# Loading the first 4096 columns of x in eight loads of every 8th partition

## The chip, the cores and the metric

The kernel runs on one core of a Trainium2 chip. The metric is device time in microseconds (us) of one execution, and lower is better. Each kernel was timed in rounds beside the kernel before on the same chip. The experiments used three chips, so their ratios are compared rather than their times.

## The reference

```python
batch, dim = 1024, 4096            # x, y: float32 (1024, 4096)
def reference(x, y, axis):         # axis = -1
    return np.sum((x - y) ** 2, axis=axis).astype(np.float32)
```

Two arrays of 16.8 MB are read, and 4 KB are written. There is one subtraction, one square and one addition for each pair of elements.

## The kernel before

Eight rows of the batch lie in each of the 128 partitions, as one line of 32,768 columns. x and y come in pieces of columns, large ones first and small ones at the end, so that little is left to compute after the last byte. VectorE (DVE in the profile) subtracts, and ScalarE (ACT) squares and sums. All loads are issued by the SyncEngine (SP), and each has a semaphore of its own.

```python
xv = x.rearrange("(p r) d -> p (r d)", p=P)        # P = 128
...
xw = [4096, 12288, 8192, 5472, 1280, 960, 320, 160]      # widths of the x loads
yw = [16256, 8192, 2624, 2784, 1344, 480, 480, 288]
...
def load(landed, src, dst, name, c0, c1):
    sem = prog.semaphore("%s%d" % (name, len(landed)))
    nc.sync.dma_start(out=dst[:, home(c0, c1)], in_=src[:, c0:c1]).then_inc(sem, 16)
    landed.append(((c0, c1), sem))
...
load(*todo.pop(0))                         # x, columns 0 to 4095
prog.early(mybir.EngineType.SP)            # ... moved ahead of the entry barrier
while todo and todo[0][5] <= H:            # H = 24576 columns of room
    load(*todo.pop(0))                     # x 12288, y 16256, x 8192, y 8192
```

`early` moves the instructions issued so far in front of the barrier at which all engines meet before the program's body. So the first load is under way while the engines still meet: its issue starts at 0.00 us and its first packet at 1.00, and the first issue behind the barrier starts at 1.43.

Of the kernel before, what the change touches and what calls it, by code (L numbers as in the profile page):

```python
# [47 lines left out]
def kernel(tc, x, y, axis, out):  # L48
    nc = tc.nc
# [10 lines left out]
    xv = x.rearrange("(p r) d -> p (r d)", p=P)  # L60
# [5 lines left out]
    X = nc.alloc_sbuf_tensor("X", [P, H], F32).ap()  # L66
# [24 lines left out]
    prog = Program(nc, tc)  # L91
# [6 lines left out]
    def home(c0, c1):  # L98
        h0 = c0 % H
        return slice(h0, h0 + c1 - c0)  # L100


    landed_x, landed_y = [], []
    freed = []

    def load(landed, src, dst, name, c0, c1):
        sem = prog.semaphore("%s%d" % (name, len(landed)))
        nc.sync.dma_start(out=dst[:, home(c0, c1)], in_=src[:, c0:c1]).then_inc(sem, 16)  # L108
        landed.append(((c0, c1), sem))
# [7 lines left out]
        order.append((landed_y, yv, Y, "y", c0, c1))  # L117

    todo = list(order)
    load(*todo.pop(0))  # L120
    prog.early(mybir.EngineType.SP)
    while todo and todo[0][5] <= H:
        load(*todo.pop(0))

# [21 lines left out]
    k = 0  # L146
# [5 lines left out]
    k = 0  # L152
# [10 lines left out]
    def wait_loaded(c1, ysem):  # L163

        waits = []
        while seen_x[0] < len(xs) and xs[seen_x[0]][0] < c1:
            waits.append(seen_x[0])
            seen_x[0] += 1
        nc.vector.wait_ge(ysem, 16)
        for k in waits:  # L170
            nc.vector.wait_ge(landed_x[k][1], 16)

    def sub(c0, c1):
        a = X[:, home(c0, c1)]
# [21 lines left out]
    for j, (c0, c1) in enumerate(ys):  # L196
        final = j == len(ys) - 1
        wait_loaded(c1, landed_y[j][1])
        for piece in pieces_of(j, c0, c1):
            sub(*piece)  # L200
            r = piece[0] // D
            if final:
                nc.vector.wait_ge(diffs, n["diffs"])
                nc.vector.tensor_tensor_reduce(  # L204
                    out=Y[:, home(*piece)],
                    in0=X[:, home(*piece)],
                    in1=X[:, home(*piece)],
                    scale=1.0,
                    scalar=parts_of(r, 1),
                    op0=mult,  # L210
                    op1=add,
                    accum_out=results[:, r : r + 1],
                ).then_inc(sums, 1)
                n["sums"] += 1
                continue
            square(*piece, where[piece])
            squared[piece] = n["acts"]
            if r in (0, 1):

                nc.sync.wait_ge(acts, n["acts"])  # L220
                while todo and todo[0][5] <= H + (r + 1) * D:
                    load(*todo.pop(0))
                if r == 1:
                    while todo:
                        load(*todo.pop(0))
# [43 lines left out]
```

## Time and profile before

| | before |
|---|---|
| median of 5 runs | 84.19 us (84.02 to 84.40) |
| span of the profiled run | 82.6 us |
| DVE, ACT busy | 45%, 40% |
| DMA queue, share of 16 engines | 95.9% |

The lines are in the prediction below. The table is to be read from its last row: the 16 DMA engines are filled nearly to the end, and the two compute engines idle for 40 us before the first large piece of y has landed. The time is the time of one stream of bytes, plus a start of 1 us and a tail of less than 3 us.

### The profile page before, as it was taken

How to read it: one execution, taken by the hardware profiler on the slowest of the kernel's cores; microseconds unless marked ns; L12 is line 12 of the kernel's file. 1: busy time of each engine (PE TensorE's matmuls, PEld its weight loads, DVE VectorE, ACT ScalarE, POOL GpSimd, SP SyncE). 2: the span in 40 equal slices, each digit the busy share in tenths (PEclk: the TensorE clock that was granted, in tenths of full speed). 3: DMA queues.
4: the chain of work that ended last, by engine and by line, in shares of the span. 5: the costliest groups of instructions: out<-in, count | busy, mean ns of one | idle time of the engine just before them, and what ended most of it. 6: DMA issues, size and time to landing. Idle time of an engine off the chain costs nothing.

```text
span 82.6 us, 136 instructions
## 1 busy us (share of the span) xinstructions
DVE 36.8 (45%) x27; ACT 33.4 (40%) x41; POOL 0.2 (0%) x4
## 2 busy tenths in 40 slices
DVE  0000000000000000000299999999189996989992
ACT  3300000000000000000000979889896999899991
POOL 0000000000000000000000000000000000000000
DMA  5998998888999991999599699969979799999960
GB/s 127 389 500 381 595 547 381 381 381 381 504 504 504 504 504 63 441 504 504 254 508 508 286 476 508 476 286 508 423 339 509 339 437 440 426 402 416 395 220 2
DMA packets 2736, 33.56 MB, mean 406 GB/s; under 512 B 432, under 2 KB 1328, under 8 KB 1712
## 3 DMA queue, kind: packets, MB, share of 16 engines
q1 hardware_dynamic: 2736, 33.56, 95.9%
HBM read 33.55 MB, written 0.00 MB: 406 GB/s over the span
## 4 chain that ended last, share of the span: by engine, by line
DMA 63%; SPq 16%; DVE 12%; ACT 4%; issue 1%
DMA Y<-in_y_dram 63%; SPq L108 16%; DVE X L175 11%; ACT X L181 4%; DVE Y L204 0%; DVE results L188 0%; SPq L220 0%; DVE results L204 0%
## 5 line engine op out<-in xcount | busy, mean ns | idle before, releaser
L175 DVE TENSOR_TENSOR X<-X,Y 128x2048 f32<-128x2048 f32 (+10 forms) x21 | 36.2, 1780 | 44.3 <-DMA Y<-in_y_dram 44.3
L181 ACT ACTIVATE X<-X 128x2048 f32<-128x2048 f32 (+9 forms) x20 | 31.2, 1559 | 46.1 <-DVE X L175 46.0
L181 ACT ACTIVATION_READ_ACCUMULATOR X<-X 128x1 f32 x20 | 3.7, 186 | 0.0
L181 ACT ACT_TABLE_LOAD x1 | 1.3, 1283 | 1.4 <-PEq L19 1.4
L188 DVE TENSOR_REDUCE results<-parts 128x1 f32<-128x2 f32 (+2 forms) x4 | 0.4, 152 | 0.0
L204 DVE CUSTOM_DVE_ANT_0 Y<-X,parts 128x128 f32<-128x128 f32 x1 | 0.4, 352 | 0.0
L250 POOL MEMSET const-bfloat16-1.0<- 128x1 bf16 x1 | 0.1, 101 | 0.0
L250 POOL MEMSET const-uint8-127<- 128x1 uint8 x1 | 0.1, 101 | 0.0
L250 POOL MEMSET const-float32-0.0<- 128x1 f32 x1 | 0.1, 98 | 0.2 <-issue 0.2
L250 POOL MEMSET const-float32-1.0<- 128x1 f32 x1 | 0.1, 98 | 0.0
L204 DVE DVE_READ_ACCUMULATOR2_ANT results<- 128x1 f32 x1 | 0.1, 83 | 0.0
## 6 DMA issues: line engine op xcount, KB each, us to landing
Y<-in_y_dram SPq DMA_DIRECT2D x1, 8128.0 KB, 39.0
X<-in_x_dram SPq DMA_DIRECT2D x1, 6144.0 KB, 20.2
X<-in_x_dram SPq DMA_DIRECT2D x1, 4096.0 KB, 48.3
Y<-in_y_dram SPq DMA_DIRECT2D x1, 4096.0 KB, 57.5
X<-in_x_dram SPq DMA_DIRECT2D x1, 2736.0 KB, 13.3
X<-in_x_dram SPq DMA_DIRECT2D x1, 2048.0 KB, 7.1
Y<-in_y_dram SPq DMA_DIRECT2D x1, 1392.0 KB, 19.0
Y<-in_y_dram SPq DMA_DIRECT2D x1, 1312.0 KB, 16.1
```

The costliest lines, as they stand in the source:

```text
L108: nc.sync.dma_start(out=dst[:, home(c0, c1)], in_=src[:, c0:c1]).then_inc(sem, 16)
L175: nc.vector.tensor_sub(out=a, in0=a, in1=Y[:, home(c0, c1)]).then_inc(diffs, 1)
L181: nc.scalar.activation(out=a, in_=a, func=Square, accum_out=acc).then_inc(acts, 1)
L188: nc.vector.tensor_reduce(out=results[:, r : r + 1], in_=parts_of(r, len(row_parts[r])), axis=mybir.AxisListType.X, op=add,).then_inc(sums, 1)
L204: nc.vector.tensor_tensor_reduce(out=Y[:, home(*piece)], in0=X[:, home(*piece)], in1=X[:, home(*piece)], scale=1.0, scalar=parts_of(r, 1), ...
L250: nc = _bacc.Bacc("TRN2", target_bir_lowering=False, num_devices=1)
```

## The change

The first x load, of 128 rows, shows in the trace of before as 128 packets of 16,384 bytes with 16 under way at a time: eight for each of 16 DMA engines. The change cuts the first x load into eight loads of 16 rows, one row (16 KB) for each engine. The intent is that an engine has its first packet, and the queue its first work, sooner. Three of the loads stand ahead of the barrier.

```diff
+    combed = [prog.semaphore("comb%d" % k) for k in range(8)]
+
+    def comb(k, c0, c1):
+        nc.sync.dma_start(out=X[k::8, home(c0, c1)], in_=xv[k::8, c0:c1]).then_inc(combed[k], 16)
...
-    load(*todo.pop(0))
+    c0, c1 = todo.pop(0)[4:]
+    landed_x.append(((c0, c1), None))
+    for k in range(3):
+        comb(k, c0, c1)
     prog.early(mybir.EngineType.SP)
+    for k in range(3, 8):
+        comb(k, c0, c1)
...
-            nc.vector.wait_ge(landed_x[k][1], 16)
+            for sem in [landed_x[k][1]] if k else combed:
+                nc.vector.wait_ge(sem, 16)
```

## The prediction

Passages are cut, and each cut is marked. They rested on rules of the hardware that no trace or run shows; the trace of before could not test them, since all its loads have 128 partitions.

> **What bounds the kernel now.** I read the page first: the slices, the DMA queue and the chain that ended last.
>
> ```profile
> span 82.6 us, 136 instructions
> DVE 36.8 (45%) x27; ACT 33.4 (40%) x41; POOL 0.2 (0%) x4
> DMA  5998998888999991999599699969979799999960
> q1 hardware_dynamic: 2736, 33.56, 95.9%
> HBM read 33.55 MB, written 0.00 MB: 406 GB/s over the span
> DMA 63%; SPq 16%; DVE 12%; ACT 4%; issue 1%
> ```
>
> The two compute engines are busy less than half of the span; the packets of the one DMA queue fill 95.9% of what 16 engines have in it. The zeros and fives in the DMA row are not pauses: packets of up to 65,024 bytes are counted in the slice where they start or end. So I asked for stretches instead (columns: stretch, its length, busy time of DVE, ACT and POOL, TensorE clock, DMA share, GB/s):
>
> ```profile
> 0.00:1.00 1.00, 0.00 (x0) 0.00 (x0) 0.20 (x4) 1.00 0.08 16
> 1.00:2.50 1.50, 0.00 (x0) 1.06 (x1) 0.00 (x0) 1.00 1.18 339
> 6.50:21.00 14.50, 0.00 (x0) 0.00 (x0) 0.00 (x0) 1.00 1.00 434
> 21.00:40.00 19.00, 0.00 (x0) 0.00 (x0) 0.00 (x0) 1.00 1.01 438
> 40.00:60.00 20.00, 17.30 (x4) 12.94 (x7) 0.00 (x0) 1.00 1.02 437
> 60.00:80.00 20.00, 18.43 (x18) 18.25 (x30) 0.00 (x0) 1.00 0.98 405
> 80.00:82.60 2.60, 1.08 (x6) 0.96 (x6) 0.00 (x0) 1.00 0.03 2
> ```
>
> The reader is to see three parts. Nothing moves in the first microsecond. Then there is a short ramp at 339 GB/s, and from there a stream at 434 to 438 GB/s that falls off only where the loads get small. The last part, 2.6 us, is the tail after the last byte. Single packet records of the trace say the same: the first packet starts 1.00 us into the span, the last of the 16 engines' first packets at 1.49; these first packets take 0.96 to 1.43 us, every later 16,384-byte packet of the first load 0.61 to 0.67, and each follows the one before it at once. The first load's last packet ends at 6.77 us, and I find no engine pausing from there to the last load's end at 79.87. The kernel is one DMA stream with a start and a tail; **what delays the stream delays the end by as much**.
>
> Last, the chain of waits in order of time, and the issues (size, time to landing):
>
> ```profile
> 1.43 0.33 SPq L108
> 1.81 39.02 DMA Y<-in_y_dram
> 53.45 0.33 SPq L108
> 66.94 13.12 DMA Y<-in_y_dram
> 80.08 0.57 DVE X L175 x2
> ...
> X<-in_x_dram SPq DMA_DIRECT2D x1, 2048.0 KB, 7.1
> ```
>
> The 2,048 KB load is the one that is changed. It does not stand in the chain by name: the chain passes from an issue at 1.43 us straight to the big y load, 39.02 us later. That is how the view draws a queue: the y load took 39 us because the first x load and a 6,144 KB load are ahead of it on the same engines. The changed load is thus on the path, through its place in the queue.
>
> [...]
>
> [...]
>
> [...]
>
> **The change part by part.** It removes one load of 128 rows x 16 KB. It adds 8 loads of 16 rows x 16 KB, three of them ahead of the entry barrier. No arithmetic changes; the listing of instruction order shows all engines but the issuing one as before.
>
> [...]
>
> Start. An issue takes 0.38 us in the first place, 0.43 to 0.44 in a row (starts 0.48 apart). The first packet at 1.00 us comes some 0.6 us after the first issue ends. With 16 rows, not 128, to describe, the spread of 0.49 us between the engines' starts may shrink. The ramp holds little: at 339 instead of 434 GB/s over 1.5 us it loses 1.5 x (1 - 339/434) = 0.33 us, most of it the cold first packets, which stay. I take **-0.15 us**.
>
> Issues. Two more loads ahead of the barrier put all three of its rounds off by 2 x 0.48, since the issuing engine is the last to come to its first round: the fourth load is issued at about 1.43 + 0.96 = 2.4 us. By then three packets per engine are queued, which last until about 1.0 + 0.65 + 3 x 0.61 = 3.5 us[...]; 2.4 + 0.6 = 3.0 is earlier. Then a load comes every 0.48 us, quicker than 0.61. The 6,144 KB load goes out near 4.8 us instead of 1.43, before the queue is empty. **0**.
>
> Completion. Seven more semaphore packets per engine: 9 ns each and about 6 to the next in the trace, 7 x 15 ns = **+0.1 us**. DVE has seven more waits ahead of its first subtraction. All of those loads land well before the y load of 39 us, whose wait stands last on that instruction: **0**.
>
> Later. DVE sits idle 40.86 us before its first subtraction; moving everything later by the same amount meets no other bound. Sum: 4.8 - 0.15 + 0.1 = +4.75 us; 84.19 + 4.75 = 88.9.
>
> **The rivals.** [...] Then only the start counts, between -0.3 and +0.1: 84.0 us. For it speaks that the kernel is finely tuned and the change's author expected a gain[...].
>
> [...]
>
> *C: the HBM side.* Neighbouring rows of one load lie 1 MiB apart (8 rows of 128 KiB). If such a step were read slower, it would add to A[...]. [...]
>
> **Range and chances.** [...] A real gain above 2% would need 1.7 us, more than the whole idle first microsecond and the ramp's 0.33, so 0.01. I predict 88.8 us and, to hold B, 86.0 to 89.6. Faster 0.01, same 0.2, slower 0.79.
>
> **What would show it.** Right: between about 1.5 and 11 us near 217 GB/s, packets of 16,384 bytes at about 1.22 us, the 6,144 KB load's packets starting near 11.3 instead of 6.55 us, and every later stretch as before but about 4.8 us later. A would show 0.61 us packets throughout and an x load done by 6.7 us. B would show 8 engines' packets at 0.61 us while the other 8 are still idle until about 3.5 us. A gap between packets of the first loads near 3 us would show that issue[...] is the bound. If the first stretch is slow and yet the end is not later, my claim that the stream has no slack is wrong.

The sum came to +4.75 us, and one of its terms, +4.8 us, was the estimate, not shown by any run at that time, that the first load would go at half rate: its 2.097 MB take 4.83 us at the measured 434 GB/s, and 9.67 at half of that. The other terms stand: -0.15 for the start, 0 for the issues, +0.1 for the completion. 84.19 + 4.75 = 88.9, put down as 88.8. Of the rivals, A says that the rate does not fall (84.0 us), and B that each load runs on half of the engines, so that the other half starts late (86.7); C is the step between the rows that are read. The chances were 0.7 for the half rate (88.3 to 89.5), 0.1 for B and a loss between (85.9 to 88), and 0.2 for A. The cuts in the expectations below have the same reason. A forecast that begins with a cut is that of the theory that the experiments test.

## The result, and the profile after

| | before | after |
|---|---|---|
| median of 5 runs | 84.19 us (84.02 to 84.40) | 89.05 us (88.94 to 89.08) |
| span of the profiled run | 82.6 us | 87.7 us |

The ratio is 1.0573, with a 95% interval of 1.0554 to 1.0592. A ratio here is the mean time of one kernel's runs over that of the other's runs of the same rounds, so it is not quite the ratio of the medians. The change made the kernel 5.7% slower.

From the page of the changed kernel:

```profile
span 87.7 us, 147 instructions
DVE 36.8 (42%) x27; ACT 33.4 (38%) x41; POOL 0.2 (0%) x4
q1 hardware_dynamic: 2848, 33.56, 95.6%
HBM read 33.55 MB, written 0.00 MB: 383 GB/s over the span
```

DVE and ACT did the same 36.8 and 33.4 us of work. The DMA queue is as full as before, 95.6%, but it moved 383 GB/s where it had moved 406. So the engines did not wait more, they were slower while busy. That is the first thing to take from these lines: *a busy share says nothing of the rate*.

The stretches show where. Their columns are the stretch, its length, busy time of DVE, ACT and POOL, TensorE clock, DMA share and GB/s. First the kernel before, from 4 to 10 us:

```profile
4.00:10.00 6.00, 0.00 (x0) 0.00 (x0) 0.00 (x0) 1.00 1.01 437
```

Then the changed kernel:

```profile
0.00:1.00 1.00, 0.00 (x0) 0.00 (x0) 0.20 (x4) 1.00 0.00 0
1.00:2.50 1.50, 0.00 (x0) 0.00 (x0) 0.00 (x0) 1.00 1.10 284
4.00:10.00 6.00, 0.00 (x0) 0.43 (x1) 0.00 (x0) 1.00 1.02 216
11.00:26.00 15.00, 0.00 (x0) 0.00 (x0) 0.00 (x0) 1.00 1.00 428
45.00:65.00 20.00, 17.30 (x4) 12.81 (x7) 0.00 (x0) 1.00 1.01 434
65.00:85.00 20.00, 18.34 (x18) 18.26 (x29) 0.00 (x0) 1.00 0.98 405
```

From 4 to 10 us the DMA share is the same 1.0, and the rate is 216 in place of 437: half. From 11 us on the numbers are those of before, five microseconds later. The view counts a packet as a whole where it falls, so a short stretch can be a few per cent off.

The chain of waits carries the same delay to the end:

```profile
6.82 39.14 DMA Y<-in_y_dram
58.58 0.33 SPq L114
72.44 12.72 DMA Y<-in_y_dram
85.18 0.57 DVE X L187 x2
```

The big y load took 39.14 us from issue to landing, and 39.02 before. But it was issued at 6.82 in place of 1.81, and so it landed 5.12 us later (45.96 against 40.84). The rest of the chain follows: the last subtractions start at 85.18 in place of 80.08. That the *issue* is late is not the cause, though it looks like it here. The y load's bytes come after those of both x loads on the same 16 engines (its first packet starts at 25.76 us, the 6,144 KB load's last at 24.49), and the experiments below that issue early and still lose show it.

Last, what the issuing engine and the barrier did (start, duration, engine, line, operation):

```profile
0.00 6.16 SPq L110 DMA_DIRECT2D X<-in_x_dram  x8
3.14 1.28 ACT L193 ACT_TABLE_LOAD   x1 [3.14 <-PEq L19]
```

ACT's table load stands right behind the barrier. It started at 1.44 us before and starts at 3.14 now: three issues of 0.57 to 0.59 us each, and a longer drain of the issuing engine (0.37 us, 0.13 before), stand in front of it.

For a finer measure I worked out, from the packet records of the traces, how many bytes had come by each moment, and when the kernel before had had as many. The difference is how far a kernel is behind; this number will be called **lag**:

| at (us) | 2.5 | 4 | 6 | 8 | 10 | 14 | 30 | 60 |
|---|---|---|---|---|---|---|---|---|
| lag of the changed kernel (us) | 0.13 | 0.81 | 1.84 | 2.79 | 3.83 | 4.81 | 4.84 | 4.91 |

It grows by half a microsecond per microsecond while the eight loads run, and stops when they are done. The last packet of all loads ends at 84.99 us in place of 79.87.

### The profile page after: what moved, and what is told of

It reads as the page before. It is cut to its first block, busy times and chain, and to the rows that moved or that the text cites. A ratio compares the mean times of both kernels' runs of the same rounds, so it can differ in the third digit from the quotient of the medians.

```text
span 87.7 us, 147 instructions
## 1 busy us (share of the span) xinstructions
DVE 36.8 (42%) x27; ACT 33.4 (38%) x41; POOL 0.2 (0%) x4
## 3 DMA queue, kind: packets, MB, share of 16 engines
q1 hardware_dynamic: 2848, 33.56, 95.6%
## 4 chain that ended last, share of the span: by engine, by line
DMA 59%; SPq 19%; DVE 11%; ACT 4%; issue 1%
DMA Y<-in_y_dram 59%; SPq L114 16%; DVE X L187 11%; ACT X L193 4%; SPq L110 3%; DVE Y L216 0%; DVE results L200 0%; SPq L232 0%; DVE results L216 0%
```

## The experiments

The theory: which partitions a load writes sets its rate, and the 16 of each of the eight loads give half. Why these should be slow together is not shown by any run. The rivals: the step of 1 MiB between the rows that are read (HBM side); the number of loads and issues; the shape of 16 rows as such; half of the engines idle at first (B of the prediction). Edits are against the changed kernel unless said otherwise. All results passed the comparison with the reference.

### Which side of the transfer

**e1_hbm_contig** reads 16 neighbouring rows of x but writes the same partitions. Its output is wrong, which doesn't matter for the time. Computed on the host, 126 sums are off by more than 0.01%, the worst by 7.7%, and the whole result by 0.9%.

```diff
-        ...(out=X[k::8, home(c0, c1)], in_=xv[k::8, c0:c1])
+        ...(out=X[k::8, home(c0, c1)], in_=xv[16 * k : 16 * k + 16, c0:c1])
```

> The eight loads still write every 8th partition, but each reads 16 neighbouring rows of x (steps of 128 KiB in place of 1 MiB); the sums are wrong on purpose. [...] nothing changes, 88.6 to 89.5 us, and packets of 16,384 bytes stay at about 1.2 us. Rival, the step of 1 MiB on the HBM side is what is read slowly: back to 84.2 to 85 us with packets near 0.61 us.

Measured: 89.03 us, ratio 1.0578 (1.0553 to 1.0604), the same as the change. The stretch from 4 to 10 us:

```profile
4.00:10.00 6.00, 0.00 (x0) 0.43 (x1) 0.00 (x0) 1.00 1.00 210
```

The HBM step falls. The same partitions written give the same half rate, whatever rows are read.

**e2_block16** takes 16 neighbouring partitions for each load, on both sides.

```diff
-        ...(out=X[k::8, home(c0, c1)], in_=xv[k::8, c0:c1])
+        p = slice(16 * k, 16 * k + 16)
+        ...(out=X[p, home(c0, c1)], in_=xv[p, c0:c1])
```

> Eight loads of 16 neighbouring partitions, both sides alike, right result. [...] HBM-step rival: 84.3. Rival that eight loads of 16 rows are slow as such: the same 89 us as the change.

The forecast gave 89.3 to 99 us, with packets near 2.4 us at the slow end.

Measured: 95.50 us, ratio 1.1345 (1.1322 to 1.1369).

```profile
4.00:10.00 6.00, 0.00 (x0) 0.00 (x0) 0.00 (x0) 1.00 1.02 128
```

The rate is 128 GB/s with all engines busy (DMA share 1.02); packets take 2.05 us, not 2.4, and the result lies in the range. Loads of the same number, rows and bytes as the change cost over twice as much extra. Neither their number nor their shape can explain that. Against e1 the pair is cleaner still: both read the same 16 neighbouring rows in each load, and only the partitions that are written differ, yet one takes 89.03 us and the other 95.50. It also shows that such a load can start as early as before: its first packet came at 0.99 us, while the changed kernel's came at 1.35.

**e12_halves** has no steps, no 16-row loads and only two issues, both ahead of the barrier (`combed` has two entries).

```diff
-        ...(out=X[k::8, home(c0, c1)], in_=xv[k::8, c0:c1])
+        p = slice(64 * k, 64 * k + 64)
+        ...(out=X[p, home(c0, c1)], in_=xv[p, c0:c1])
...
-    for k in range(3):
+    for k in range(2):
         comb(k, c0, c1)
     prog.early(mybir.EngineType.SP)
-    for k in range(3, 8):
-        comb(k, c0, c1)
```

> Two loads, partitions 0 to 63 and 64 to 127, both ahead of the barrier: no step, no 16-row loads, few issues. [...] half rate for both loads, 88.4 to 89.0 us. [...] each load would have 8 engines of its own and both would run side by side: 84.2 to 84.8 us.

The 84.2 to 84.8 us are those of rival B.

Measured: 89.26 us, ratio 1.0607 (1.0591 to 1.0623), a little above the range.

```profile
4.00:10.00 6.00, 0.00 (x0) 0.00 (x0) 0.00 (x0) 1.00 0.99 208
```

With 64 rows and two issues the loss is that of the change, so few rows, steps and many issues are all unnecessary for it. Rival B falls here: with half of the engines for each load, the two would have run side by side. And a late issue is not needed either, since the big y load was issued at 2.88 us, not at 6.82.

**e10_every2nd** is the same two loads, but of every 2nd partition.

```diff
-        p = slice(64 * k, 64 * k + 64)
-        ...(out=X[p, home(c0, c1)], in_=xv[p, c0:c1])
+        ...(out=X[k::2, home(c0, c1)], in_=xv[k::2, c0:c1])
```

(This diff is against e12_halves.)

> Two loads of every 2nd partition, 64 rows each, both ahead of the barrier. [...] there is work for 5 us from two issues. What is left is the cost of a step between partitions: the first packet at 1.3 in place of 1.0 us. 84.4 to 84.7 us. If a step as such slows the packets: 86 or more.

Measured: 84.51 us, ratio 1.0045 (1.0030 to 1.0060).

```profile
4.00:10.00 6.00, 0.00 (x0) 0.00 (x0) 0.00 (x0) 1.00 1.06 453
```

This pair has as many loads, rows, bytes and issues, and takes 89.26 against 84.51 us. Only which partitions make up a load differs, and with them the rows that are read; e1 and e2 hold those fixed. What is left, 0.4 us, is a later start: its first packet begins at 1.33 us in place of 1.00, and its lag is 0.37 us from 4 us to the end. That isolates the start as a cost. A step between partitions, which the expectation names as its reason, is not needed for it: the first packet of e12, which has no step, came at 1.34 us.

### How much, and in what order

**e9_double** gives the eight loads 8192 columns.

```diff
-    xw = [4096, 12288, 8192, 5472, 1280, 960, 320, 160]
+    xw = [8192, 8192, 8192, 5472, 1280, 960, 320, 160]
```

> The change with 8192 columns in its eight loads in place of 4096, and so many fewer in the next load: packets of 32 KB, which[...] take 2.4 us, far longer than the 0.63 us from one issue to the next, so that no engine waits for an issue. [...] 9.0 to 9.7 us, and 0.35 us for the start: 93.3 to 94.3 us. A cost of the eight issues or of the start alone: 89.

The 9.0 to 9.7 us are about twice the extra time of the half rate in the change; the 2.4 us of a packet are twice the change's 1.2.

Measured: 94.91 us, ratio 1.1271 (1.1250 to 1.1291): 10.8 us over before, where the change has 4.9. The cost goes with the bytes. It is 0.6 us more than the range, because a packet at half rate is slower than I had it: 32,768 bytes take about 2.55 us, which is 12.8 GB/s for an engine. That is less than half of the 27.1 that an engine has in the trace of before (49,152 bytes in 1.815 us).

```profile
4.00:10.00 6.00, 0.00 (x0) 0.43 (x1) 0.00 (x0) 1.00 1.01 208
```

**e6_half** was to be the other end of this line.

```diff
-    xw = [4096, 12288, 8192, 5472, 1280, 960, 320, 160]
+    xw = [2048, 14336, 8192, 5472, 1280, 960, 320, 160]
```

> Only the first 2048 columns come in the eight loads (8 KB packets); the next load takes 2048 columns more, so the bytes are the same. [...] half the bytes at half rate, 2.4 us in place of 4.8, and the same late start of 0.35 us: 86.8 to 87.4 us. A fixed cost of having eight such loads would leave 89.0.

Measured: 88.28 us, ratio 1.0513 (1.0470 to 1.0557), over 0.8 us too slow for half the loss and not the fixed cost either. The trace says why it is no test:

```profile
3.55:4.43 0.88, 0.00 (x0) 0.88 (x1) 0.00 (x0) 1.00 0.00 0
```

For 0.88 us nothing moves. Three packets of 8 KB per engine are used up long before the fourth load, which is issued behind the barrier at 3.15 us, has its first packets at 4.44; and later each issue (0.63 us from one to the next) is slower than a packet. Here the issues *are* a bound. In the changed kernel they were not, because there each packet took 1.2 us.

**e5_alternate** changes the order, so that loads of k = 0 to 3 and of k = 4 to 7 take turns.

```diff
-    for k in range(3):
+    for k in (0, 4, 1):
...
-    for k in range(3, 8):
+    for k in (5, 2, 6, 3, 7):
```

> The change with its eight loads in the order 0, 4, 1, 5, 2, 6, 3, 7[...]. [...] in the change this shows as a hump of about 230 GB/s over 207 near 6.5 us. Seven switches in place of one give 0 to 1.5 us: 87.5 to 88.9 us. [...] the order could not matter: 89.0.

A switch is a passage between those two groups. That there is time to gain at one was an estimate from the trace of the change: 229 GB/s from 6 to 7 us, where its one switch falls, and 197 from 8 to 9.5. The 89.0 us are those of the rival, that the order does not matter.

Measured: 88.19 us, ratio 1.0482 (1.0463 to 1.0501): 4.1 us over the kernel before on its chip, where the change has 4.9, and in the range. The order of equal loads matters, which no theory of counts gives.

```profile
4.00:10.00 6.00, 0.00 (x0) 0.43 (x1) 0.00 (x0) 1.00 1.07 273
```

### Between: other ways to cut the load

**e4_every4th** has four loads of every 4th partition (three early, `combed` has four entries).

```diff
-        ...(out=X[k::8, home(c0, c1)], in_=xv[k::8, c0:c1])
+        ...(out=X[k::4, home(c0, c1)], in_=xv[k::4, c0:c1])
-    for k in range(3, 8):
+    for k in range(3, 4):
```

> Four loads of every 4th partition, 32 rows, two packets for each engine[...]. [...] 87 to 89 us. [...] 84.2 to 84.8 us. HBM-step rival (steps of 512 KiB): 84.3.

The first two forecasts rest on guesses that no run shows: 87 to 89 us if the loads go at half rate, 84.2 to 84.8 if at the full one.

Measured: 85.51 us, ratio 1.0156 (1.0135 to 1.0176), between these two. From 2.5 to 4 us most packets take 0.61 us, the time of before, so the loads go at the full rate there. But some pause near 4.4 us, and packets of 0.7 to 1.6 us follow. Its lag is 0.2 us at 4 us and 0.96 from 10 us on; the engines are then out of step, and the last of them ends 1.56 us later than before.

**e7_every4th_one_early** was to show that the barrier is behind the pause.

```diff
-    for k in range(3):
+    for k in range(1):
-    for k in range(3, 4):
+    for k in range(1, 4):
```

(This diff is against e4_every4th.)

> The four loads of every 4th partition, with one of them ahead of the entry barrier in place of three. In the run with three, some engines pause near 4.5 us and rates of 340 to 380 GB/s follow, about 1 us in all. If the pause comes from the barrier, which three issues put off, and the late fourth load: 84.4 to 84.9 us. If it comes from loads of this shape as such: 85.5 as with three.

Measured: 85.88 us, ratio 1.0214 (1.0170 to 1.0258). The expectation of a gain failed. The trace shows another pause in place of the first: the second load, issued at 1.84 us behind the barrier, has its first packet at 3.3 us, when the first load's packets are mostly done. One early load is too little work, and with three something else makes engines pause. What that is stays open.

**e3_cols8** cuts by columns, with all partitions in each load.

```diff
-        ...(out=X[k::8, home(c0, c1)], in_=xv[k::8, c0:c1])
+        w = (c1 - c0) // 8
+        c0, c1 = c0 + k * w, c0 + (k + 1) * w
+        ...(out=X[:, home(c0, c1)], in_=xv[:, c0:c1])
```

> Eight loads again, three of them ahead of the barrier, but each of all 128 partitions and 512 of the columns[...]. [...] 84.3 to 85.2 us (2,048-byte packets cost about 0.5 us over the load, the semaphores 0.1). Rival, that the number of loads and their issue is the cost: near 89 us. It also tells whether the later first packet (1.35 in place of 1.00 us) belongs to loads of 16 rows or to the wait of three issues.

The 0.5 us are an estimate: in the trace of before a packet of 1,920 bytes takes 0.079 us, so 64 of 2,048 bytes take 5.4 us, where 8 of 0.61 us take 4.9.

Measured: 86.93 us, ratio 1.0319 (1.0289 to 1.0348), a miss of 1.7 us. It isn't the half rate: packets of 2,048 bytes take 0.08 us where they are undisturbed. But from 2.4 us on many take 0.1 to 1.4, with pauses between, and engines fall out of step; the lag is 2.0 us from 12 us on, and the last engine ends 2.6 us late.

**e8_cols8_one_early** puts one of them ahead of the barrier.

```diff
-    for k in range(3):
+    for k in range(1):
-    for k in range(3, 8):
+    for k in range(1, 8):
```

(This diff is against e3_cols8.)

> The eight loads of 128 partitions and 512 columns, with one ahead of the barrier in place of three. If the 2.7 us of the run with three come from engines left without work at the late fourth load: 84.6 to 85.6 us. If they come from many loads with small packets at the cold start: 86.5 to 87.5.

Measured: 86.46 us, ratio 1.0277 (1.0247 to 1.0306), at the edge of the second case. So the barrier accounts for little of the 2.7 us. Cutting the first load into small ones has a cost of its own at this place, which I have measured and not explained. It does not add up with the half rate in any simple way: e12, with two large loads, lost as much as the change with eight.

**e11_step7** keeps 16 rows and eight loads, but seven of them take every 7th partition and the last takes 16 neighbours.

```diff
-        ...(out=X[k::8, home(c0, c1)], in_=xv[k::8, c0:c1])
+        p = slice(k, k + 106, 7) if k < 7 else slice(112, 128)
+        ...(out=X[p, home(c0, c1)], in_=xv[p, c0:c1])
```

> Seven loads of every 7th partition, 16 rows each, and one of the last 16 partitions: right result, as many loads, rows and issues as the change[...]. [...] gives +2.8 to +3.1 us over the kernel before[...] (it gives +4.7 to +4.9 for the change); with 0.35 us for the start 86.6 to 87.6 us. [...] 89.0 as in the change.

The first forecast, 86.6 to 87.6 us, is from a model that no run shows; the 89.0 are for the case that it is wrong.

Measured: 89.13 us, ratio 1.0579 (1.0557 to 1.0602). The expectation failed by 1.5 us, and the time is the other one that it gave, 89.0. The trace shows that it is not the same loss, though:

```profile
4.00:10.00 6.00, 0.00 (x0) 0.45 (x1) 0.00 (x0) 1.00 1.07 273
```

The change has 216 here. Three things make up the time. The packets of the second load all take 0.78 to 0.96 us, where the model had most at 0.61 and a few at 1.22. Engines run dry between 4 and 5 us, since the fourth load is issued at 3.16 us behind the barrier, and again near 7.5 us: from 2 to 8 us each engine is without a packet for 0.85 us on average, against 0.04 in the change; the forecast had no term for such waits. And the last load, of 16 neighbours, brings the rate down to 175 to 190 GB/s from 9 to 10.5 us. The last two are flaws of the experiment. The first is not: every 7th partition did not give nearly the full rate. So the model failed.

The cause stays open here. The runs show how long a packet of 16 KB takes for the partitions of its load: 0.61 us for every 4th (e4), 0.78 to 0.96 for every 7th, 1.19 on average and 1.27 in the last round for every 8th (the change), 2.05 for 16 neighbours (e2). The packet records hold time and size, but no partition, so no trace shows why.

## Why the prediction was right

**The stream.** That a delay of the stream delays the end by as much held: the lag was 4.84 us at 30 us and 4.91 at 60, and the time rose by 4.86.

**The half rate.** The step that carried the prediction, and an estimate when it was made. Between 2.5 and 14 us the lag grew by 4.81 - 0.13 = 4.7 us; the prediction had 4.8. e1 ruled out the HBM step, e2 and e12 the counts and shapes, and e1 against e2 and e12 against e10 left the choice of partitions alone. In the third and the last two of eight rounds the packets take 1.26 to 1.27 us on average and not 1.22. What brought the mean of the first load's 128 packets back to 1.19 are shorter packets at the start (from 0.74 us) and in the fifth round, where the loads pass from k = 3 to k = 4 (1.09 to 1.17). The engines had drifted apart by the end: the 6,144 KB load's packets, forecast near 11.3 us, began between 10.52 and 11.68 (6.55 to 6.77 before). What the runs do *not* show is why these partitions together are slow; the one model that was tried failed in e11.

**Start.** This term had the wrong sign: -0.15 us predicted. The first packet began at 1.35 us, not earlier than 1.00. Of these 0.35 us, 0.20 are the longer issue (0.58 us in place of 0.38); the rest is not explained. Over all runs the first issue took 0.37 to 0.38 us for 128 rows or 16 neighbours, and 0.54 to 0.60 for 64 neighbours or rows with a step; the first packet then came 1.32 to 1.39 us after its start in place of 0.99 to 1.00. Yet the lag at 2.5 us is only 0.13 us; the first packets, 0.74 to 1.28 us each (0.96 to 1.43 before), made up for the rest. The intent of the change failed at this point even without the half rate, as e10 shows with its 0.4 us.

**Issues.** Right in effect (0), wrong in size: the fourth load went out at 3.13 us and not at 2.4, since the early issues start 0.62 us apart, not 0.48, and the drain is longer. The half rate hid this. At the full rate it would not have been hidden: e6, with 8 KB packets, shows the dry queue.

**Completion.** The extra waits of DVE cost nothing: the first subtraction starts 0.02 us after the landing of y, as before (45.96 to 45.98). The semaphore packets, predicted at +0.1, cost less: they overlap the data packets, and from 2.2 to 10 us each engine is without a data packet for 0.04 us on average.

**The rivals.** A (no loss of rate) fell with e12 and e10. B fell with e12, and in the changed kernel itself 16 packets were under way at once. C fell with e1.

**The sum.** 88.8 us predicted (its own terms add to 88.94), 89.05 measured, in the range of 86.0 to 89.6. The start term was 0.28 us too low in lag, the half-rate and completion terms each up to 0.1 too high, and the engines end less evenly than before (the last packet is 5.12 us later, the bulk 4.9). That the sum comes within 0.3 us is partly luck, since these errors cancel; that nearly all of it is the half-rate term is not. One slip of reading, on which nothing rests: two of the first load's later packets before took 0.68 and 0.88 us, not 0.67 at most.

## What to carry to other kernels

Before cutting a load by partitions, look at which partitions each piece has, and measure its rate: a load of 64 neighbouring partitions ran at half rate (208 GB/s from 4 to 10 us), one of every 2nd partition at the full one (453). A queue that is full and busy at half its rate looks healthy in a busy share (95.6% here, 95.9% before), so read GB/s by stretch. And a first load that is already back to back has only its start to give; count that microsecond before adding issues in front of a barrier.
